# A rotary embedding of 16 heads on one core: the first tile's loads on a second DMA queue, the last store in two pieces

## The chip, the cores and the metric

The kernel runs on one core of one Trainium2 chip. A core has five engines that run side by side, each with its own instruction stream: TensorE (PE), VectorE (DVE), ScalarE (ACT), GpSimd (POOL) and SyncE (SP). Sixteen DMA engines move data between the chip's main memory (DRAM) and the on-chip memory. The metric is the device time of one execution in microseconds (us), taken as the median of several runs.

## The reference

The input x has 16 batches, 512 positions and 16 heads of 64 numbers, all float32; sin and cos have 512 x 32 numbers. Each head's vector is cut into two halves of 32, which are rotated by the position's angles:

```python
x1, x2 = (x[..., :half_dim].copy(), x[..., half_dim:].copy())
rotated = np.concatenate([x1 * cos - x2 * sin, x1 * sin + x2 * cos], axis=-1)
```

Every output number is the sum of two products: its own input times cos, and its partner's input (from the other half) times plus or minus sin. The input is 33.6 MB and so is the output.

## The kernel before

The work is cut into eight tiles of two batches each. A tile is 128 partitions by 8192 numbers, 4 MB: partition p of a batch holds 8 consecutive positions, which the program calls rows 0 to 7, of 1024 numbers each. A tile lives in one of five buffers (`BUFS = 5`), is loaded by one DMA transfer (`load`, line 70), changed in place, and stored from the same buffer (`store`, line 76). Both are issued by SyncE.

At the start (lines 80 to 92) SyncE issues, in this order: the first piece of tile 0 (rows 0 to 2, `FIRST[0]` is 3), the sin table, the cos table, the second piece of tile 0 (rows 3 to 7), and the whole tiles 1 to 4. After them come five transfers of 64 bytes each into a small tile called `spare`, whose contents nothing reads. The completion of a transfer is told by one of eight semaphores, which are taken in turn; a transfer is issued only when the earlier one on the same semaphore has landed. So the number of spare transfers sets which earlier transfer each later load or store waits for.

The tables come in on 64 partitions. TensorE spreads them to 128 by a product with a doubled identity (lines 113 and 114), and VectorE makes from them `sns`, the sines with their signs (lines 116 and 117), and a small table of row 0's own (line 119). No row can be worked on before that.

The loop from line 201 on takes tile by tile; the order of work on each engine is the order in which the lines stand, since the schedule is written by hand. The eight rows go three ways:
- Rows 1 and 2, 4 and 5, 6 and 7 go in pairs. VectorE multiplies a pair by cos into a PSUM tile (`pair_product`, line 141), GpSimd multiplies its swapped halves by the signed sines (`sin_rows`, line 165), and VectorE adds the two back into the tile (`pair_sum`, line 189).
- Row 3 has its sine product from GpSimd, too; TensorE adds it to VectorE's cosine product (`pe_half`, line 176), and ScalarE copies the sum back (line 181).
- Row 0 has both products from VectorE (lines 141 and 150), the sum from TensorE, and the copy back from ScalarE (line 209).

GpSimd's order within a tile is: rows 1 and 2, row 3, rows 4 and 5, rows 6 and 7. VectorE's is: the cosine product of rows 1 and 2, row 0's sine product, the addition of rows 1 and 2, half of row 3, the product of rows 4 and 5, their addition, the other half of row 3, the product of rows 6 and 7, row 0 of the next tile, and the addition of rows 6 and 7.

After each tile it is stored (`stores`, line 191). `LAST_OUT = (8,)` says where the last tile's store is cut: it isn't, all eight rows go in one transfer. Tiles 5 to 7 are loaded into the buffers of tiles 0 to 2; SyncE issues these loads after the store of tile 2, each when its buffer's store has landed.

Of the kernel before, what the change touches and what calls it, by code (L numbers as in the profile page):

```python
# [8 lines left out]
FP32 = mybir.dt.float32  # L9
# [10 lines left out]
PAIRS = ((1, 2), (4, 5), (6, 7))  # L20

FIRST = (3, 8)
LAST_OUT = (8,)

EXTRA = 5


@with_exitstack
def kernel(
# [13 lines left out]
    nc = tc.nc  # L43
# [6 lines left out]
    KK = seq // PB  # L50
# [3 lines left out]
    x_v = x.rearrange("(t b) (p k) d -> t (b p) (k d)", b=NB, k=KK)  # L54
    out_v = out.rearrange("(t b) (p k) h d -> t (b p) (k h d)", b=NB, k=KK)
    cos_v = cos.rearrange("(p k) j -> p (k j)", k=KK)
    sin_v = sin.rearrange("(p k) j -> p (k j)", k=KK)

    fixed = ctx.enter_context(tc.tile_pool(name="fixed", bufs=1))
# [7 lines left out]

    tiles = [None] * NT

    def load(t, lo=0, hi=KK):  # L70
        if tiles[t] is None:
            tiles[t] = xp.tile([P, F], FP32, name="xt")
        s = slice(lo * dim, hi * dim)
        nc.sync.dma_start(out=tiles[t][:, s], in_=x_v[t][:, s])  # L74

    def store(t, lo=0, hi=KK):
        s = slice(lo * dim, hi * dim)
        nc.sync.dma_start(out=out_v[t][:, s], in_=tiles[t][:, s])

    load(0, 0, FIRST[0])  # L80
    tabs = bp.tile([P, 2 * dim], FP32, name="b")
    sin_sb = tabs[:PB, : KK * half]
    cos_sb = tabs[:PB, dim : dim + KK * half]
    nc.sync.dma_start(out=sin_sb, in_=sin_v)
    nc.sync.dma_start(out=cos_sb, in_=cos_v)
    for lo, hi in zip(FIRST, FIRST[1:]):
        load(0, lo, hi)
    for t in range(1, BUFS):
        load(t)
    spare = fixed.tile([1, EXTRA, 16], FP32)  # L90
    for i in range(EXTRA):
        nc.sync.dma_start(out=spare[:1, i], in_=sin_v[:1, :16])

    ident = fixed.tile([P, P], FP32)
    make_identity(nc, ident)
# [4 lines left out]
    for ps in (own_ps[:, :BANK], own_ps[:, BANK:], pe_ps):  # L100
# [9 lines left out]
        out=spread.rearrange("p (b q) -> p b q", b=NB),  # L110
        in_=bass.AP(tensor=eye.tensor, offset=eye.offset, ap=[eye.ap[0], [0, NB], [1, PB]]),
# [79 lines left out]
    def stores(t):  # L191
        lo = 0
        for hi in LAST_OUT if t == NT - 1 else (KK,):
            store(t, lo, hi)
# [64 lines left out]
```

## Time and profile before

| | |
|---|---|
| median of 9 runs | 162.36 us (162.17 to 162.85) |
| the profiled execution | 162.36 us |
| its span, first to last instruction | 160.6 us |
| DVE busy | 136.3 us (85%) |
| POOL busy | 127.1 us (79%) |
| PE busy | 57.7 us (36%) |
| ACT busy | 18.1 us (11%) |
| DMA | 67.25 MB, mean 419 GB/s |

The profile is of one execution. It gives each engine's busy time, its times in 40 equal slices of the span (a 9 is a slice with 90% or more), the DMA queues with their bytes, and groups of instructions by source line, with what ended the idle time ahead of them. In a line of the timeline the first number is the start and the second the duration in us, then engine, line, operation, and in brackets the idle time before it. "SPq" is SyncE's queue, which issues transfers; q1 is the DMA queue that SyncE's transfers go through, and q14 one that fetches instructions. A DMA engine's share of a transfer consists of packets; here a packet is one partition's part of it, up to 32 KB.

### The profile page before, as it was taken

To read this page: it belongs to the slowest core of one execution; us is meant where nothing else is said; L and a number is where in the kernel's file an instruction comes from. 1 tells how busy PE (TensorE), PEld (TensorE's weight loads), DVE (VectorE), ACT (ScalarE), POOL (GpSimd) and SP (SyncE) were. 2 spreads that over 40 slices of the span, in tenths; PEclk is the share of its full clock that TensorE was granted. 3 is DMA by queue.
4 is the path that set the end of the run, shared out by engine and by line. 5 is a ranking of instruction groups with operands and counts; after the bars stand their busy time and mean duration, and the time that the engine had idled before them with its cause. 6 is when DMAs were issued, how large, how long until landed. Compare 5 with 4: busy or idle time off the path is not lost.

```text
span 160.6 us, 443 instructions
## 1 busy us (share of the span) xinstructions
PE 57.7 (36%) x71; PEld 19.2 (12%) x71; DVE 136.3 (85%) x85; ACT 18.1 (11%) x25; POOL 127.1 (79%) x38
## 2 busy tenths in 40 slices
PE   3041915055503831091408250655047411913000
PEld 0021301021101210031003010211022101310000
DVE  1059969999999999999999999999999999999000
ACT  0001321003010301012100310031003010211000
POOL 1039999999999999988998899898998899850000
PEclk9999995558555765568555955585557655685555
DMA  5999999999999999999999999999999999999994
GB/s 171 411 413 473 392 465 449 392 416 498 392 408 490 408 392 498 416 392 490 427 392 441 465 400 408 482 408 408 482 416 400 490 416 400 490 408 408 392 441 212
DMA packets 2619, 67.25 MB, mean 419 GB/s; under 512 B 314, under 2 KB 442, under 8 KB 442
## 3 DMA queue, kind: packets, MB, share of 16 engines
q1 hardware_dynamic: 2618, 67.24, 98.0%
q14 instruction: 1, 0.01, 0.0%
HBM read 33.69 MB, written 33.55 MB: 419 GB/s over the span
## 4 chain that ended last, share of the span: by engine, by line
DVE 68%; issue 12%; POOL 6%; DMA 4%; PE 1%; SPq 0%; DVEq 0%
DVE xt L189 33%; DVE pd L141 31%; POOL b L165 6%; DMA b<-in_sin_dram 4%; DVE pe_ps L141 3%; PE tab L113 1%; PE tab L114 1%; DVE sns L116 0%; DVE xt L150 0%; DVE own_ps L141 0%; SPq L74 0%; DVE sns L117 0%; DVEq L189 0%
## 5 line engine op out<-in xcount | busy, mean ns | idle before, releaser
L165 POOL TENSOR_TENSOR b<-xt,sns 128x2048 f32<-128x2048 f32 (+1 forms) x32 | 126.4, 3977 | 14.8 <-DVE sns L117 9.3
L189 DVE TENSOR_TENSOR xt<-pd,b 128x2048 f32<-128x2048 f32 x24 | 54.9, 2287 | 2.4 <-POOL b L165 1.6
L141 DVE TENSOR_TENSOR pd<-xt,tab 128x2048 f32<-128x2048 f32 x24 | 55.0, 2291 | 0.2
L176 PE MATMUL own_ps<-xt,ident 128*128 128x512 f32 x32 | 29.9, 1091 | 54.0 <-DVE xt L150 48.3
L176 PE MATMUL pe_ps<-b,ident 128*128 128x512 f32 x32 | 25.8, 899 | 27.9 <-DVE pe_ps L141 27.9
L176 PEld LDWEIGHTS own_ps<-xt,ident 128*128 128x128 f32 x32 | 9.4, 324 | 74.0 <-DVE xt L150 59.3
L209 ACT COPY xt<-own_ps 128x1024 f32<-128x1024 f32 x8 | 8.1, 1012 | 73.0 <-PE own_ps L176 73.0
L181 ACT COPY xt<-pe_ps 128x512 f32<-128x512 f32 x16 | 9.4, 588 | 39.8 <-PE pe_ps L176 39.8
L176 PEld LDWEIGHTS pe_ps<-b,ident 128*128 128x128 f32 x32 | 8.4, 292 | 43.4 <-DVE pe_ps L141 34.9
L141 DVE TENSOR_TENSOR pe_ps<-xt,tab 128x512 f32<-128x512 f32 x16 | 11.0, 686 | 0.0
L141 DVE TENSOR_TENSOR own_ps<-xt,tab 128x1024 f32<-128x1024 f32 x8 | 9.8, 1224 | 0.0
L150 DVE TENSOR_TENSOR xt<-xt,tab 128x1024 f32<-128x1024 f32 x8 | 9.7, 1214 | 0.0
L116 DVE TENSOR_SCALAR sns<-tab 128x256 f32<-128x256 f32 x1 | 0.4, 424 | 8.3 <-PE tab L114 8.3
L209 ACT ACT_TABLE_LOAD x1 | 1.3, 1283 | 15.5 <-DVE xt L150 15.5
L113 PE MATMUL tab<-b,spread 64*128 64x256 f32 x2 | 1.2, 696 | 5.1 <-DMA b<-in_sin_dram 5.1
L101 PE MATMUL own_ps<-zero 128*128 128x512 bf16 x2 | 1.0, 621 | 1.2 <-DVE zero L97 1.2
L113 PEld LDWEIGHTS tab<-b,spread 64*128 64x128 f32 x2 | 0.5, 306 | 6.0 <-issue 6.0
L114 PE MATMUL tab<-b,spread 64*128 64x256 f32 x2 | 1.1, 631 | 0.0
L97 DVE MEMSET zero<- 128x256 uint32 x1 | 0.3, 272 | 0.9 <-PEq L240 0.9
L114 PEld LDWEIGHTS tab<-b,spread 64*128 64x128 f32 x2 | 0.7, 333 | 0.2
L101 PE MATMUL pe_ps<-zero 128*128 128x512 bf16 x1 | 0.6, 634 | 0.0
L101 PEld LDWEIGHTS <-zero 128*128 128x128 bf16 x3 | 0.3, 124 | 1.5 <-DVE zero L97 1.2
(9 smaller groups left out, 1.8 us busy)
## 6 DMA issues: line engine op xcount, KB each, us to landing
out_dram<-xt SPq DMA_DIRECT2D x8, 4096.0 KB, 21.2
xt<-in_x_dram SPq DMA_DIRECT2D x7, 4096.0 KB, 39.0
xt<-in_x_dram SPq DMA_DIRECT2D x1, 2560.0 KB
xt<-in_x_dram SPq DMA_DIRECT2D x1, 1536.0 KB
spare<-in_sin_dram SPq DMA_DIRECT2D x5, 0.1 KB
b<-in_sin_dram SPq DMA_DIRECT2D x1, 64.0 KB
b<-in_cos_dram SPq DMA_DIRECT2D x1, 64.0 KB
```

Source lines behind the costliest of these rows:

```text
L97: nc.vector.memset(zero, 0.0)
L101: nc.tensor.matmul(out=ps, lhsT=zero[:, :P], rhs=zero, start=True, stop=True)
L113: nc.tensor.matmul(out=sin_t, lhsT=spread, rhs=sin_sb, start=True, stop=True)
L114: nc.tensor.matmul(out=cos_t, lhsT=spread, rhs=cos_sb, start=True, stop=True)
L116: nc.vector.tensor_scalar_mul(out=sns[:, :, 0, :], in0=sin_k, scalar1=-1.0)
L141: nc.vector.tensor_tensor(out=o, in0=i, in1=cb, op=ALU.mult)
L150: nc.vector.tensor_tensor(out=heads(r), in0=heads(r), in1=s, op=ALU.mult)
L165: nc.gpsimd.tensor_tensor(out=o, in0=i, in1=sb, op=ALU.mult)
L176: nc.tensor.matmul(out=ps, lhsT=ident, rhs=other, start=False, stop=True, skip_group_check=True)
L181: nc.scalar.copy(out=r, in_=pe_ps)
L189: nc.vector.tensor_tensor(out=r, in0=ps, in1=b, op=ALU.add)
L209: nc.scalar.copy(out=r0, in_=own_ps)
```

## The change

SyncE issues sin first, then cos, then tiles 1 to 4. The two pieces of tile 0 are issued by ScalarE. The spare transfers become four, of 2, 4, 5 and 6 rows of 64 bytes. The store of the last tile is cut after row 3 into two transfers. The work of the engines on the data is the same.

```diff
-LAST_OUT = (8,)
-
-EXTRA = 5
+LAST_OUT = (4, 8)
+
+EXTRA = (2, 4, 5, 6)
...
-    def load(t, lo=0, hi=KK):
+    def load(t, lo=0, hi=KK, queue=nc.sync):
         if tiles[t] is None:
             tiles[t] = xp.tile([P, F], FP32, name="xt")
         s = slice(lo * dim, hi * dim)
-        nc.sync.dma_start(out=tiles[t][:, s], in_=x_v[t][:, s])
+        queue.dma_start(out=tiles[t][:, s], in_=x_v[t][:, s])
...
-    load(0, 0, FIRST[0])
     tabs = bp.tile([P, 2 * dim], FP32, name="b")
     sin_sb = tabs[:PB, : KK * half]
     cos_sb = tabs[:PB, dim : dim + KK * half]
     nc.sync.dma_start(out=sin_sb, in_=sin_v)
+    load(0, 0, FIRST[0], nc.scalar)
     nc.sync.dma_start(out=cos_sb, in_=cos_v)
     for lo, hi in zip(FIRST, FIRST[1:]):
-        load(0, lo, hi)
+        load(0, lo, hi, nc.scalar)
     for t in range(1, BUFS):
         load(t)
-    spare = fixed.tile([1, EXTRA, 16], FP32)
-    for i in range(EXTRA):
-        nc.sync.dma_start(out=spare[:1, i], in_=sin_v[:1, :16])
+    spare = fixed.tile([16, len(EXTRA), 16], FP32)
+    for i, n in enumerate(EXTRA):
+        nc.sync.dma_start(out=spare[:n, i], in_=sin_v[:n, :16])
```

## The prediction

> **What bounds the kernel now.** I read the page's slices first, then stretches, the chain, the timeline at both ends, and last the DMA packets. The page:
>
> ```profile
> DVE  1059969999999999999999999999999999999000
> ...
> DMA  5999999999999999999999999999999999999994
> ...
> q1 hardware_dynamic: 2618, 67.24, 98.0%
> ```
>
> The 16 DMA engines are full from the second slice to the last but one: 67.24 MB through the one queue q1 take 98% of the span. VectorE (DVE) is as solid, from slice 3 until 12 us before the end. The stretches say the same (us, engine busy times and counts, TensorE clock, DMA share, GB/s):
>
> ```profile
> 10.65:30.40 19.75, 7.22 (x8) 2.31 (x8) 18.14 (x12) 3.46 (x4) 19.75 (x5) 0.83 1.04 445
> 30.40:148.30 117.90, 46.94 (x56) 15.46 (x56) 116.82 (x70) 14.62 (x21) 106.70 (x28) 0.60 1.00 431
> ```
>
> From 30.40 to 148.30 DVE (third pair) is busy 116.82 of 117.90 us: a delay of tile 0 is never caught up, but moves the end of DVE by its full size. The chain, at the start:
>
> ```profile
> 1.17 6.42 DMA b<-in_sin_dram
> ...
> 10.65 3.30 POOL b L165
> 13.95 1.17 issue
> 15.12 6.85 POOL b L165 x2
> 21.99 2.29 DVE xt L189
> ```
>
> Compute starts at 10.65, when the tables have come, been spread by TensorE and copied. GpSimd (POOL) takes rows 1 and 2 until 15.12, then row 3 (2.33 us), then rows 4 and 5 (4.52 us). At 21.99 DVE adds the latter and from there has no gap. So 15.12 is when the second piece of tile 0 (rows 3 to 7) is wanted first; it landed at 13.87 by the trace's semaphore records. The first piece landed at 7.28, sin at 7.60, cos at 7.90, tile 1 at 23.6. The other end, in the timeline:
>
> ```profile
> 145.88 0.58 ACT L181 COPY xt<-pe_ps 128x512 f32<-128x512 f32 x1 [4.72 <-PE pe_ps L176]
> 146.01 2.29 DVE L189 TENSOR_TENSOR xt<-pd,b 128x2048 f32<-128x2048 f32 x1
> 148.37 0.33 SPq L78 DMA_DIRECT2D out_dram<-xt  x1
> ```
>
> The last store is issued at 148.37; the span ends at 160.57, 12.2 us later. Its packets begin at 149.20; on most engines the store before had ended at 148.6 to 149.2, but on the slowest, whose last packet ends the transfer at 159.4, it ended at 149.73. So DVE and DMA arrive together: the last engine never idles, and the others 0.2 to 0.5 us. Neither can lose two microseconds without moving the end.
>
> **What the Trainium skill says.** (1) In the Trainium skill, "DMA: Bandwidth & Descriptors", section "Queues, rings and completion order": SyncE (SP) and ScalarE (ACT) each own one queue row, with a ring on each of the same 16 engines; an engine goes round-robin between rows that have work, at the boundaries of packets, which it calls typically 9 to 17 descriptors; completion is not first-in-first-out. (2) The same page, "SWDGE vs HWDGE vs iDMA", gives a packet as preferably at most 4096 B. The two leave open how much one turn is here, and everything hangs on that: a whole transfer, or one row's descriptor. The trace helps. An instruction fetch came through q14 amid a tile's store; in the half microsecond around it, the queues' packets:
>
> ```profile
> q1 hardware_dynamic: 16, 0.52, 125.1%
> q14 instruction: 1, 0.01, 1.9%
> ```
>
> By its record that packet (8 KB, 0.309 us) ran from 79.73 to 80.04. On one engine a 32 KB store packet had ended at 79.74, and the eighth and last packet of that engine's share of the same store began at 80.04. So another row got its turn inside a transfer, after the seventh packet of eight, and the engine served one packet at a time. I take one 12, 20 or 32 KB packet as the turn. Only one small packet shows it, and priority for fetches isn't excluded. (3) The same page, "Issuing engines are not separate DMA queues": a second issuing engine saves sequencer time only, no transfer time; q1's 98% agrees, there is nothing to add.
>
> **The change, part by part.** Packet times are from the trace: 1 KB 0.046 us, completion write 0.009, 12 KB 0.460, 20 KB 0.766, 32 KB 1.213. Each engine has 4 packets of a table, 8 of each tile piece or tile, and one completion write per transfer.
>
> *Issue at the head.* SP issues sin at 0.73 in place of the first piece, cos at about 1.2, and tile 1 at about 1.8 (now: 0.44 and 0.58 us between issues) rather than near 2.9, as two x issues have left it. ACT issues the two pieces from about 0.73; it has nothing to do before 15.48. Its queue has no row in this trace: bound its first packet by SP's (1.77, 1.04 us after issue) and 0.7 us later. By itself this costs nothing: ACT's two issues, about 1 us, lie in its idle time before 15.48; without that they would delay its first copy by as much.
>
> *What the pieces now run beside.* Today one ring is in order: piece 1, tables, piece 2, tile 1. Afterwards tiles 1 to 4 stand in SP's ring behind the tables and take turns with the pieces in ACT's. Up to the completion of piece 2, ACT's ring needs 8+1+8+1 = 18 turns. Between them SP's ring gets 17 or 18. The first 10 are the tables' (2 x (4+1)), cheap; the other 7 or 8 are packets of tile 1, 1.213 us each. Sum: start 1.77; piece 1 8 x 0.460 = 3.7, plus about 0.8 for the slow first packets (now 0.5 to 1.4 us); piece 2 8 x 0.766 = 6.1; tables 8 x 0.046 + 2 x 0.009 = 0.4; tile 1 7.5 x 1.213 = 9.1; landing after the last packet about 0.45 (as now). Piece 2 lands at 22.3.
>
> *The tables.* Interleaved so, sin lands after some five packets of piece 1 and cos after ten turns, about 7.5 (now 7.90): compute starts near 10.3, a gain of at most 0.4, or about 3 if the tables run wholly ahead; then piece 1 lands near 10. Neither matters: POOL would finish rows 1 and 2 by about 15 at the latest and wait for piece 2.
>
> *The stall.* POOL's row 3 goes from 15.12 to 22.3: 7.2 us. Behind it on POOL stand rows 4 and 5; DVE's row-3 product waits for the same piece, its addition of rows 4 and 5 for POOL. DVE's 1.58 us gap before 21.99 is already behind POOL in both. Everything from 21.99 shifts by 7.2. Tile 1 then lands near 23, wanted at 34.
>
> *The tail.* The first half of the last tile (rows 0 to 3) is ready when ACT's copy ends, 145.88 + 0.58 = 146.46, so it is issued at 146.53 against 148.37 now: 1.84 us sooner. The second half follows at 148.37, while the first still moves (4.85 us). An additional issue (0.34 us) and 16 KB packets in place of 32 KB cost under 0.1: 12 KB packets run at 26.7 GB/s, 32 KB at 27.0. Today the split would gain nearly nothing, since the slowest engine is busy until 149.73; after a stall, all 1.84.
>
> *Spares.* Four in place of five, and more rows each: 64 B rows, at most 0.1 us on any engine. They keep the order of the eight completion semaphores, taken in turn: the first store, which now waits at 33.3 for tile 2's landing, would wait for tile 1's, and the later loads for nothing new. SP's third spare wait now ends with cos, its fourth with piece 2 at 22.3; SP is next wanted at 37.6. Zero, covered by that 15 us.
>
> *Sum.* First half issued at 146.53 + 7.2 = 153.7; plus 12.2 to the span's end: 165.9. By then the DMA engines have emptied (the seventh store would be done near 150), so nothing is queued ahead. The profiled execution takes 162.36 for a span of 160.6, 1.8 around it, and equals the median: 165.9 + 1.8 = **167.7 us**.
>
> **Rivals.**
> A. *The tables don't absorb the turns.* If sin, or both tables, pass before piece 1 reaches the engines, tile 1's packets take their turns: with sin gone 11 or 12 of them, piece 2 lands near 27, the stall is about 12, and the time 172. With both gone, some 15 or 16 turns, 31: 176. For: sin is small and first. Against: the first packets are slow to start, so piece 1 probably arrives while sin is still on its way.
> B. *Equal bytes for both rings.* Until tile 1 arrives near 2.7, 0.25 MB of piece 1 are done; the rest 1.32 x 2 / 0.433 = 6.1 us, piece 2 2.62 x 2 / 0.433 = 12.1: landed at 21.4, stall 6.3, time 166.8. Practically the same forecast.
> C. *Not slower: a turn is a whole transfer* (or the older goes first). Then piece 1, cos, piece 2 pass before tile 1, piece 2 lands near 13.5, nothing stalls, and compute starts up to 2.5 us earlier. That gain ends at the DMA engines, which are full; left is what the tables cost amid q1 today, as piece 2's first packets behind them took 1.1 us instead of 0.77: 0.0 to 0.5 us. Time 162.1. For: the first of the Trainium skill's packet sizes. Against: the fetch between packets seven and eight. It decides up to a landing of piece 2 near 17: the split forgives a stall of 1.84, and a little more on the slowest engine.
> D. *A small stall*, ACT's packets getting more than every second turn: 163 to 165.5.
>
> **How the numbers follow.** Forecast with B 0.45 (the likeliest, own range 165.5 to 169), A 0.27 (0.20 near 172, 0.07 near 176), D 0.08, C 0.20. The range leaves out 176 and the edge of C: 161.7 to 173.5. A measurement of this kernel tells about 0.2%, 0.33 us: C gives 0.11 faster, 0.09 same; the rest is slower, 0.80.
>
> **What would show it.** Right: packets of two queues mixed from 2 us; POOL's row 3 of tile 0 waiting for x until about 22; DVE's gap there about 9 instead of 1.58; DVE's end near 155.5; a slice of DMA below full before the last store; the two last issues 1.84 us apart. Wrong: piece 2 landing before 17, or DVE catching up in the middle. A landing near 27 means A.

## The result, and the profile after

The changed kernel takes 163.88 us (median of 10 runs, 163.54 to 164.13) against 162.35 for the kernel before, a ratio of 1.0089 (95% interval 1.0078 to 1.0099). It is slower, clear of the noise and as forecast, but by 1.5 us where 5.3 were forecast, and by another path than the forecast one. The profiled execution took 164.13 us with a span of 162.3.

The page of the changed kernel, slices and queues (q10 is the queue of ScalarE's transfers):

```profile
DVE  1006996999999999999999999999999999999400
...
DMA  5999999999999998998998999999999999996796
...
q1 hardware_dynamic: 2498, 63.05, 90.4%
q10 hardware_dynamic: 288, 4.19, 6.7%
```

DVE begins a slice later, and near the end the DMA engines are no longer full (the 6 and the 7 ahead of the last 9). The chain of the changed kernel at the start:

```profile
1.33 11.01 DMA b<-in_cos_dram
...
14.41 0.07 issue
14.48 1.89 POOL b L165
16.37 2.59 issue
18.95 6.85 POOL b L165 x2
25.80 0.02 issue
25.83 2.29 DVE xt L189
```

The piece called "issue" at 16.37 is no idle time: in the chain GpSimd's product stands only up to the landing of the second piece, for which the next one waits. The timeline has eight products in one block:

```profile
14.48 31.52 POOL L165 TENSOR_TENSOR b<-xt,sns 128x2048 f32<-128x2048 f32 x8 [13.18 <-DVE sns L117]
```

GpSimd's first product now starts at 14.48 instead of 10.65, since cos, issued 0.4 us earlier than before, lands only at 12.34 by the semaphore records (7.90 before). From there everything is as it was, 3.83 later: row 3 is taken at 18.95 without a wait, as the second piece has landed at 16.29, and the addition stands at 25.83 instead of 21.99. VectorE's last addition ends at 152.14 (148.30 before), also 3.84 later: nothing is caught up between. The other end, in the timeline:

```profile
149.71 0.58 ACT L181 COPY xt<-pe_ps 128x512 f32<-128x512 f32 x1 [4.70 <-PE pe_ps L176]
149.85 2.29 DVE L189 TENSOR_TENSOR xt<-pd,b 128x2048 f32<-128x2048 f32 x1
150.32 2.18 SPq L78 DMA_DIRECT2D out_dram<-xt  x2
```

The first half of the last tile goes out at 150.32, 1.95 us after the whole tile did before, and the span ends 12.0 us after it. In stretches of the end (the pairs are busy time and count of TensorE's products, its weight loads, VectorE, ScalarE and GpSimd; the last three columns are TensorE's granted clock, the DMA engines' share and GB/s):

```profile
145.00:147.40 2.40, 0.00 (x0) 0.00 (x0) 2.40 (x2) 0.01 (x1) 1.36 (x1) 0.91 0.98 423
147.40:150.00 2.60, 2.07 (x2) 0.50 (x2) 2.50 (x3) 0.29 (x1) 0.00 (x0) 0.50 0.50 214
```

From 147.4 to 150.0 the DMA engines are half idle: the seventh store has run out and the last tile isn't ready. So far: a late table, 3.83, less the 1.84 that the split gives back, which makes 1.99. The two profiled executions differ by 1.77, the medians by 1.5; what the sum has too much is of the size by which single executions differ (163.54 to 164.13).

**Why cos is late** is in the records of the DMA packets. On one engine (an engine's packets are told apart by one's end and the next one's start; S is SyncE's ring, A ScalarE's, with the start in us and the size):

```
1.74 A 12 KB   2.88 A   3.40 A   3.87 A   4.33 A   4.79 A
5.24 S 1 KB    5.29 A 12 KB   5.74 S 1 KB   5.79 A 12 KB   6.24 S 1 KB   6.28 A completion   6.29 S 1 KB
6.33 A 20 KB   7.11 S completion   7.12 A 20 KB   7.91 S 1 KB   7.96 A 20 KB   8.76 S 1 KB   8.80 A 20 KB
9.62 S 1 KB    9.67 A 20 KB   10.52 S 1 KB   10.56 A 20 KB   11.39 S completion   11.39 A 20 KB
12.17 S 32 KB  13.38 A 20 KB  14.14 S 32 KB  15.36 A completion
```

The rings take turns by single packets, and a completion write is a turn. But they do so only from 5.24 on: six packets of the first piece went ahead of sin's first. The tables' ten turns therefore fall mostly among the 20 KB packets of the second piece, each of which costs cos some 0.8 us; and since the tables fill ten of the twelve turns that SyncE's ring gets, only two packets of tile 1 come in ahead of the second piece's completion.

### The profile page after: what moved, and what is told of

Read it like the earlier page. It is cut to its first block, busy times and chain, and to the rows that moved or that the text cites. A ratio compares the mean times of both kernels' runs of the same rounds, so it can differ in the third digit from the quotient of the medians.

```text
span 162.3 us, 443 instructions
## 1 busy us (share of the span) xinstructions
PE 58.2 (36%) x71; PEld 19.1 (12%) x71; DVE 136.3 (84%) x85; ACT 18.1 (11%) x25; POOL 127.1 (78%) x38
## 4 chain that ended last, share of the span: by engine, by line
DVE 67%; issue 13%; DMA 7%; POOL 5%; PE 1%; SPq 0%; DVEq 0%
DVE xt L189 32%; DVE pd L141 31%; DMA b<-in_cos_dram 7%; POOL b L165 5%; DVE pe_ps L141 3%; PE tab L114 1%; SPq L83 0%; DVE sns L116 0%; DVE xt L150 0%; DVE own_ps L141 0%; DVE sns L117 0%; DVEq L189 0%
```

## The experiments

The theories. *Turns*: as just read, a late table by way of turns, a shift of the whole, part of it given back by the split. *Queue*: the second queue, or SyncE's handing over, is itself slow. *Ahead*: six packets went first because an engine has accepted several packets of a busy ring when another ring's first one arrives; its rival, *start*, is that this delay belongs to the beginning of the program.

### The split taken out

```diff
-LAST_OUT = (4, 8)
+LAST_OUT = (8,)
```

> The changed kernel with its last tile stored whole again. If the shift of 3.8 us at the head runs through to the end and the split gives back 1.84 of it: 163.9 + 1.8 = 165.7 us. If the split gives nothing, because the DMA engines are busy until then anyway: 163.9.

Measured: 165.92 us, ratio 1.0202 (1.0181 to 1.0222) to the kernel before, 2.04 more than the changed kernel. Without the split the loss, 3.5 us, is nearly the whole shift of 3.83; the split is worth its head start of 1.84 once compute is late.

### The split alone

```diff
 (kernel before)
-LAST_OUT = (8,)
+LAST_OUT = (4, 8)
```

> The kernel before with its last tile stored in two pieces and nothing else. Theory (the slowest DMA engine is busy until the store begins): 162.2 to 162.5, no difference. Rival (the half stored 1.84 us earlier is worth its time): 160.5 to 161.

Measured: 162.51 against 162.48, ratio 1.0002 (0.9987 to 1.0016). With compute on time the split is worth nothing.

### The second piece back on SyncE

```diff
 (changed kernel)
-        load(0, lo, hi, nc.scalar)
+        load(0, lo, hi)
```

> The changed kernel with the second piece of tile 0 issued by SyncE again, behind cos; only the first piece goes through ScalarE's queue. Theory (cos is late because its packets take turns with the 20 KB packets of the second piece): cos lands by about 8.5 us instead of 12.3, compute starts near 10.7, the DMA engines alone set the end, 162.2 us (161.9 to 162.5). Rival (it is the second queue as such, or SyncE's late start, that delays the tables): cos still lands after 11 and the time stays near 163.9.

Measured: 162.53 us, ratio 1.0008 (0.9996 to 1.0019); cos landed at 8.00. The timeline's start of GpSimd and the two last issues:

```profile
10.72 20.25 POOL L165 TENSOR_TENSOR b<-xt,sns 128x2048 f32<-128x2048 f32 x5 [9.42 <-DVE sns L117]
...
146.52 2.18 SPq L78 DMA_DIRECT2D out_dram<-xt  x2
```

With the second piece behind cos in the same ring the whole loss is gone, though the first piece still goes through ScalarE's queue. So the loss is the meeting of cos with the second piece, not the second queue. The four larger spare transfers and the split store are in this kernel too, and the time is that of the kernel before: neither costs anything here.

### All on one queue, tables first

```diff
 (changed kernel)
     nc.sync.dma_start(out=sin_sb, in_=sin_v)
-    load(0, 0, FIRST[0], nc.scalar)
     nc.sync.dma_start(out=cos_sb, in_=cos_v)
+    load(0, 0, FIRST[0])
...
-        load(0, lo, hi, nc.scalar)
+        load(0, lo, hi)
```

> All on SyncE's one queue in the order sin, cos, first piece, second piece, tiles; spares and split store as changed. Theory: tables land near 3 us, compute starts when the first piece lands, 7.3 to 7.7, then waits for the second piece at about 13.9, one us ahead of the kernel before; the DMA engines set the end: 162.2 us (161.8 to 162.4). Rival (an earlier compute start is worth its time): 161 or less.

Measured: 164.19 us, ratio 1.0094 (1.0073 to 1.0115). The tables landed by 3.67 and GpSimd started at 8.79, 1.9 us ahead of the kernel before; yet the time is 1.8 longer, which neither theory expected. A stretch of this kernel at the start, and GpSimd's second wait:

```profile
1.77:3.30 1.53, 1.06 (x4) 0.22 (x2) 0.00 (x0) 0.00 (x0) 0.00 (x0) 1.00 0.69 149
...
14.81 18.06 POOL L165 TENSOR_TENSOR b<-xt,sns 128x1024 f32<-128x1024 f32 x5 [1.51 <-DMA xt<-in_x_dram]
```

Until 3.30 only the tables move, 149 GB/s: the first packet of x starts at 3.16 instead of 1.77. Part of that comes back, since the tables needn't be moved later: tile 1 lands at 24.46 instead of 23.58, 0.88 late. Another 0.9 is lost near 51.5, where one packet of tile 4 on each engine took 1.76 to 2.23 us instead of 1.21: tile 4 lands at 54.50 instead of 52.73, and the slowest engine ends 1.86 later than before. So only half of the loss is the order at the head; why those packets were slow stays open. Nor is this a clean test of an earlier start, since GpSimd waits again at row 3 for the second piece, and begins it at 14.81, only 0.3 us ahead of the kernel before. In the changed kernel the first packet of x comes at 1.74, as ScalarE issues the first piece beside sin.

### The queues exchanged

```diff
 (changed kernel: sin and cos by ScalarE, all of x by SyncE)
-    nc.sync.dma_start(out=sin_sb, in_=sin_v)
-    load(0, 0, FIRST[0], nc.scalar)
-    nc.sync.dma_start(out=cos_sb, in_=cos_v)
+    nc.scalar.dma_start(out=sin_sb, in_=sin_v)
+    load(0, 0, FIRST[0])
+    nc.scalar.dma_start(out=cos_sb, in_=cos_v)
...
-        load(0, lo, hi, nc.scalar)
+        load(0, lo, hi)
```

> The changed kernel with the queues exchanged: ScalarE issues sin and cos, SyncE all of x. Theory (what counts is that tables and pieces stand in different rings): sin's first packet near 5 us, cos landed near 12, compute starts near 14.5, time 163.9 (163.5 to 164.2). Rival (SyncE is slow to hand over small transfers): tables land by 4 us, time 162.3.

At the head this is as *Turns* has it: six packets of the first piece, then turns; sin's first packet at 5.15, cos landed at 12.23, GpSimd started at 14.36. It made no difference there which engine issued the tables and which the pieces. The time, 162.97 us (ratio 1.0038, 1.0021 to 1.0055), is 0.9 below the changed kernel, and the reason lies elsewhere. The same stretch of the end, of this kernel:

```profile
147.40:150.00 2.60, 1.13 (x2) 0.30 (x2) 2.50 (x2) 0.59 (x1) 0.00 (x0) 0.83 0.50 214
150.00:152.00 2.00, 0.00 (x0) 0.00 (x0) 1.99 (x1) 0.00 (x0) 0.00 (x0) 0.50 1.13 475
```

TensorE was granted 0.83 of its clock there instead of 0.50, so the last two products of row 3 took 1.13 us instead of 2.07, and the first half was issued at 149.22 instead of 150.32. In both kernels row 3's products decide when the half is released, and how long they took went with the granted clock in that stretch.

### Cut after row 2

```diff
 (changed kernel)
-LAST_OUT = (4, 8)
+LAST_OUT = (3, 8)
```

> The changed kernel with the last tile cut after row 2, not row 3: the first part then needs nothing of TensorE's late second half of row 3. Theory (the changed kernel ends when it does because its first part is released at 150.3, when the DMA engines have run dry): rows 0 to 2 are released at about 144.5, follow the seventh store without a gap, rows 3 to 7 follow at 152.2, and the end comes at 160.4 to 160.9, time 162.2 to 162.7. Rival (the late end of VectorE costs its time wherever the cut is): 163.9.

Measured: 162.90 us, ratio 1.0038 (1.0023 to 1.0053), just above the expected range. The issues and stretches of this kernel:

```profile
144.36 8.04 SPq L78 DMA_DIRECT2D out_dram<-xt  x2
...
147.40:150.00 2.60, 1.12 (x2) 0.30 (x2) 2.50 (x3) 0.59 (x1) 0.00 (x0) 0.78 0.98 418
```

The DMA engines stay full through the stretch in which they were half idle, with VectorE as late as before: 1.0 of the 1.5 us comes back. The rest is with one DMA engine, whose last packet ended at 159.89 (159.41 for the slowest one of the kernel before), while the others were done by about 159.2. What holds that engine up wasn't settled. The time is no better than that of the exchanged queues (162.97), where the cut stayed after row 3 and TensorE had the higher clock: the cut after row 2 gave about what that clock gave, but its first part doesn't wait for TensorE's late products at all.

### A newcomer among 32 KB packets

```diff
 (kernel before)
+    probe = fixed.tile([PB, 2, KK * half], FP32)
...
         nc.scalar.copy(out=r0, in_=own_ps)
+        if t in (2, 5):
+            nc.scalar.dma_start(out=probe[:, t // 5], in_=sin_v)
```

> The kernel before with two more transfers of the sin table (64 rows of 1 KB, into a tile that nothing reads), issued by ScalarE in tiles 2 and 5, while SyncE's ring is full of 32 KB packets. Theory 1 (an engine has accepted several packets of the busy ring ahead, so a newcomer waits for them): the first packet comes about 7 us after the issue if six packets are ahead, about 2.7 us if 72 KB are ahead; then one packet per 1.22 us. Theory 2 (the tables' 3.4 us delay belongs to the start of the program): first packet within 1 to 2.2 us of the issue, then one per 1.22 us, landed after about 6 us. In both the time stays within 0.2 us of the kernel before.

One execution took 162.66 us. ScalarE issued at 54.36 and 105.33; by the packet records the first packets of the 16 engines came at 59.08 to 59.52 and at 109.19 to 110.54, so 4.7 to 5.2 and 3.9 to 5.2 us after the issue. Afterwards they were about 1.25 apart, one of SyncE's 32 KB packets between; where SyncE's turn was a completion write, the next came after some 0.05 us. The DMA view of the first stretch, from the issue to 59.0, has packets of SyncE's queue alone (the last line gives the transfer's size and its 9.3 us from issue to landing):

```profile
q1 hardware_dynamic: 59, 1.93, 95.2%
...
probe<-in_sin_dram ACTq DMA_DIRECT2D x1, 64.0 KB, 9.3
```

The same table on empty engines (in the one-queue kernel) had its first packet 1.33 us after the issue. So the wait behind a busy ring isn't a matter of the start: *start* falls. Both figures under *Ahead* were off, and both had left out the 1.33 us that a first packet takes without a busy ring: a wait of some 3.5 us more is about three packets of 32 KB (96 KB), where six of 12 KB (72 KB) went ahead at the start. So it isn't a fixed number of packets. As times the waits from issue to first packet lie close together, 4.4 us for sin in the changed kernel and 3.9 to 5.2 here; whether bytes or a time set them, these points don't tell.

### The first piece a little later

```diff
 (changed kernel; the memset of zero is moved ahead)
+    late = fixed.tile([P, 16], BF16)
...
     nc.sync.dma_start(out=sin_sb, in_=sin_v)
+    nc.scalar.copy(out=late, in_=zero[:, :16])
     load(0, 0, FIRST[0], nc.scalar)
```

> The changed kernel with a small copy (and the load of ScalarE's function table that it needs) ahead of ScalarE's two issues, so that the first piece is issued near 2.3 us and meets tile 1's packets, with the tables gone ahead. Theory (one packet per ring and turn, and a newcomer waits some 4.5 us from its issue behind what an engine has accepted): first packet near 6.8, first piece landed near 20, second near 37.7 (17 packets of tile 1 between, 1.213 us each), a stall of 22.6, time 183 us (178 to 187). Rival (rings share bytes equally): second piece at 26 to 27, time 172.

Measured: 167.54 us, ratio 1.0315 (1.0289 to 1.0341). The edit didn't do what it was made for: ScalarE's queue issued at 1.17, while the function table was still loading, and the copy ran only at 2.03:

```profile
0.73 1.28 ACT L87 ACT_TABLE_LOAD   x1 [0.73 <-PEq L242]
...
1.17 0.85 ACTq L74 DMA_DIRECT2D xt<-in_x_dram  x2
...
2.03 0.20 ACT L87 COPY late<-zero 128x16 bf16<-128x16 bf16 x1
...
22.34 11.28 POOL L167 TENSOR_TENSOR b<-xt,sns 128x1024 f32<-128x1024 f32 x3 [6.53 <-DMA xt<-in_x_dram]
```

So the first piece was late by 0.45 us alone, and neither figure expected applies. It still tells much: sin had passed when the first piece came (landed at 3.44), cos hadn't. Six packets of the first piece went first again; then cos took five turns, and tile 1 seven. The second piece landed at 22.27, and GpSimd waited 6.53 us for it: the stall that the prediction had in mind, with other causes. 0.45 us in one issue cost 3.7 us of time.

### Three pieces

```diff
 (changed kernel)
-FIRST = (3, 8)
+FIRST = (3, 4, 8)
```

> The changed kernel with row 3 of tile 0 as a piece of its own (4 KB packets), rows 4 to 7 as the third (16 KB packets), all by ScalarE. Theory (one packet per turn, whatever its size): the tables' ten turns fall on the end of the first piece and on row 3's small packets, cos lands near 8; compute starts near 10.5; rows 4 to 7 then take turns with tile 1 (0.61 + 1.21 us each) and land near 22.3 where 17.4 is wanted: a stall of 4.9, time 165.3 (164.3 to 166.3). Rival (the loss of the change is the late table alone): 162.3.

Measured: 169.02 us, ratio 1.0392 (1.0362 to 1.0423). cos landed at 8.64 and GpSimd started at 10.78, as expected: beside 4 KB packets turns are cheap. But the third piece landed at 26.00, not at 22.3, so the stall is 8.6. The transfer in the chain, and GpSimd's wait in the timeline:

```profile
1.61 24.39 DMA xt<-in_x_dram
...
26.16 8.97 POOL L165 TENSOR_TENSOR b<-xt,sns 128x2048 f32<-128x2048 f32 x2 [8.55 <-DMA xt<-in_x_dram]
```

I had counted 8 turns of tile 1; the records show eleven turns: the eight packets of tile 1, its completion write and two packets of tile 2.

**One count for three kernels.** Leave out the six packets that go ahead, and give SyncE's ring one turn for each of ScalarE's that is left (8 packets and one completion write per piece, on each engine): 18 - 6 = 12 turns in the changed kernel, ten of the tables and 2 of tile 1; 12 again with the later first piece, five of cos and 7 of tile 1; 27 - 6 = 21 with three pieces, ten of the tables and 11 of tiles 1 and 2. The packet records of these kernels show 2, 7 and 11. This was put together after the runs; no run was made to test it on a fourth case.

### Spares of one row

```diff
 (changed kernel)
-EXTRA = (2, 4, 5, 6)
+EXTRA = (1, 1, 1, 1)
```

> The changed kernel with its four spare transfers of one row each, as the kernel before has them. Theory (only their number counts, for the turn of the completion semaphores): 163.9 us (163.6 to 164.1). Rival (the rows matter): anything outside that.

Measured: 163.98 us (163.0 to 164.16), ratio 1.0088 (1.0053 to 1.0122). These runs show no effect of the rows of the spare transfers.

## Why the prediction was wrong

Slower was right, but for another reason than the one given: the stall that was forecast didn't come, and the loss came from a table that the prediction had put at nothing.

- **One packet per turn:** right. The choice between the two packet sizes in the Trainium skill ("DMA: Bandwidth & Descriptors", sections "Queues, rings and completion order" and "SWDGE vs HWDGE vs iDMA") went the way that the one instruction fetch pointed (the lines shown there are of a window of one microsecond, half on either side of the fetch). A turn is one packet of the records, of 1 to 32 KB, or one completion write by itself. If such a record is one descriptor, the 9 to 17 descriptors of the first section aren't seen here, and neither is the second section's 4096 B; that section gives the figure where it tells how GpSimd's descriptors are built, and GpSimd issues no transfer here. Equal bytes (rival B) and whole transfers (rival C) are both out by the packet records.
- **"The first 10 are the tables'", interleaved from the start:** this is the step that failed. ScalarE's ring needed its 18 turns, but SyncE's got 12 between them, not 17 or 18: six packets of the first piece passed before sin's first packet, at 5.17 rather than 1.8. I had put the second queue's start-up at 0 to 0.7 us on ScalarE's side and none on SyncE's. On empty engines sin's first packet takes 1.33 us from its issue, the piece's 1.02. That these 0.3 us decide who goes ahead fits the kernel with the later first piece, in which sin went first; why a ring that comes second then waits some 3 us more stays open.
- **Piece 2 at 22.3:** 16.29 was measured. The term of 7.5 packets of tile 1 was 2: with six turns gone, the tables absorbed ten of the twelve that were left. A landing before 17 was named as a sign of being wrong, and it was one.
- **"Neither matters" of the tables:** wrong, by the same six packets. cos landed at 12.34 where 7.5 was forecast, and compute started at 14.48 where 10.3 was forecast.
- **The stall of 7.2:** there was none at row 3; in its place stands a shift of 3.83 at the very first product.
- **Rival D** (ScalarE's packets get more than every second turn, 163 to 165.5 us, chance 0.08) has the measured time in its range and fits what the first six packets did. But it too looked for a stall at the second piece; that piece came 1.2 us after 15.12, and nothing waited for it, as compute was late by more.
- **A shift is never caught up:** right, 3.83 at GpSimd's start and 3.84 at VectorE's end.
- **The tail:** right. 1.84 was forecast for the split after a stall and nearly nothing without one; 2.04 and nothing were measured. The sum with the true shift holds: 146.53 + 3.83 = 150.36, issued at 150.32; plus 12.2 makes 162.5 for a span of 162.3. It holds because the last two products of row 3 ran at a clock of 0.50 in both kernels (2.08 us before, 2.07 after); at the clock of the exchanged queues the half would have gone out a microsecond sooner. The prediction had not considered the clock, so that part is luck.
- **Rival A** was the right worry with the wrong size: with sin passed, 11 or 12 packets of tile 1 and 172 us were put down; the later first piece showed 7 and 167.5, again for the six packets ahead.
- **Rival C's bound**, that an earlier start of compute is worth nothing, isn't settled. On one queue GpSimd started 1.9 us earlier and the time was longer, but it waited again for the second piece, and the DMA engines had lost time of their own.

## What to carry to other kernels

In these kernels a second DMA queue was no free parallel path. While both rings were full, each engine alternated between them packet by packet, so a small transfer paid one of the other ring's packets for each of its own on an engine (0.8 us beside 20 KB, 1.2 beside 32 KB), and a transfer that used to be next in line shared with whatever the other ring held. Put what must come first into one ring, in the order in which it is wanted; where two rings run side by side, count turns (packets and completion writes), not bytes. Small tables ahead of the first large load aren't free either: in one ring they put tile 1 back by 0.88 us. Where DMA and one engine end together, look at what the first part of a split last store depends on: cut after row 2 it was issued at 144.36 instead of 150.32, and no longer waited for TensorE's last products.

## What was not expected of the hardware

- A transfer on a second queue got its first packet some 3 to 4 us later beside a busy ring than on empty engines: 4.4 us after the issue beside 12 KB packets and 3.9 to 5.2 beside 32 KB packets, against 1.33.
- ScalarE's queue issued DMAs at 1.17 although a copy that stands ahead of them in its own program only ran at 2.03.
- With the same shift at the head, the end differed by 1.1 us of span between two kernels, as TensorE's last two products took 1.13 or 2.07 us at a granted clock of 0.83 or 0.50 in that stretch.
